# Transposing DMAs at steps 1 and 3, their joins at 5 and 7, in a mixture-of-experts block on one core

## The chip, the cores and the metric

The kernel runs on one core of a Trainium2 chip. The metric is the device time of one execution, in microseconds (us). PE is the matrix engine (its weight loads are listed apart, as PEld), DVE the vector engine, ACT the scalar engine, POOL the GpSimd engine. SP is a sequencer that here only issues DMAs; the rows of the profile call it SPq. All five run their own instructions in order and wait for each other through semaphores.

## The reference

One layer of a generator over 2048 tokens of width 1024, in float32: a short gated convolution mixer and a mixture of experts with expert-choice routing.

```python
hl = modulate(rms_norm(lat, norm_g[i, 0]), sh1, sc1)
gate_b, gate_c, v = jnp.split(hl @ w_in, 3, axis=-1)
lat = lat + g1 * ((gate_b * dwconv_centred(gate_c * v, conv_w)) @ w_out)
h = modulate(rms_norm(lat, norm_g[i, 1]), sh2, sc2)
...
cap = EC_CAPACITY_FACTOR * N // N_EXPERTS                 # 2 * 2048 // 16 = 256
aff = jax.nn.softmax((h @ w_router).astype(jnp.float32), axis=-1)
g, idx = lax.top_k(jnp.swapaxes(aff, 1, 2), cap)          # each of 16 experts takes 256 tokens
xs = h[idx]
hid = jax.nn.silu(xs @ w_gate) * (xs @ w_up)
ys = (hid @ w_down) * g                                    # added back to the chosen tokens' rows
lat = lat + g2 * scatter_add(ys, idx)
```

## The kernel before

**Arithmetic.** Every product is made of float32 operands that are split into a rounded high part and the rest (`ws[:, 0]` and `ws[:, 1]` for weights, `xT[:, 0]` and `xT[:, 1]` for tokens); high x high, high x low and low x high are three matmuls. ACT makes a high part by a copy (L200), DVE the low part by a subtraction (L210).

**The weight chain.** All weights go through one queue of pieces of 512 KB, in a fixed order: `load_to` issues the load of a piece on SP into one of three raw buffers (L184), `split_high` is ACT's copy, `split_low` DVE's subtraction, and `split_low(i)` then calls `load_to(i + 3)`, so a load goes out when the piece three before it has been split. A split piece stands in one of eight `ws` buffers until PE has used it.

**The output stage** (about 580 to 830 us) goes over 16 blocks of 128 tokens. Between the matmuls of block tb + 1, `behind(tb, k)` places the work on block tb at step k of 8: residual and norm at 0, transposition for the router at 4 and 5, `out_h2` at 5, `router_mm` at 7; the router's sum over halves (`router_sum`, a small PE product, L727) follows at step 0 of the next block. `out_h2` finishes a row block `u` of h on DVE and calls `halves_out`: ACT copies `u` apart into its 16-bit halves (L683) and SP stores them to `hhalf`, from which experts 1 to 15 gather. `router_mm` ends with ACT's copy of the router's sums out of PSUM into `lt` (L722), which `router_sum` reads.

**The experts** (from 880 us). Expert e runs as `gate_up(e, 0)`, `down(e - 1, 0)`, `gate_up(e, 1)`, `down(e - 1, 1)`: half of the hidden columns each, and the down products of the expert before between them. A `gate_up` has eight steps k (24 matmuls of 256 columns each, with one weight piece split for later), a `down` four steps kk (12 matmuls of 512 columns, one piece split). `gate_up` ends with silu on ACT (L1054), the product on DVE (L1055) and the split of the result; PE's next `gate_up` but one uses the same PSUM banks.

Tokens for expert e + 1 come in four pieces of work, which are placed at steps by the `between` functions:

- `pick_oh` and `pick`: from the chosen slots DVE builds a one-hot table, PE multiplies it (16 small matmuls), DVE makes the row numbers `idx`, and POOL issues two gathers of 128 rows each into `xs` (L984).
- `turn(e, s)`: SP issues a transposing DMA of half s of the tokens, `tr <- xs` (L1012). The buffer of half 1 is that of the one-hot table.
- `join(e, s)`: DVE copies one 16-bit half and ACT the other into `full` (L1018, L1019), ACT makes the high part of `xT` (L1022), DVE the low part (L1023).

Within a step of `gate_up` the order is: ACT's split of the step's piece, then `between(k)`, then DVE's split, which issues the next load. What is placed by `between` therefore stands on SP ahead of that load, and on ACT and DVE between two splits.

Of the kernel before, what the change touches and what calls it, by code (L numbers as in the profile page):

```python
# [20 lines left out]
E = 16  # L21
# [20 lines left out]
def block_kernel(ctx: ExitStack, tc, x, c, ada_w, ada_b, norm_g, w_in, conv, w_out, router, wg, wu, wd, out):  # L42
# [307 lines left out]
    with tc.tile_pool(name="mix", bufs=1) as mix:  # L350
# [7 lines left out]
        def hl_tile(shape, dt=F32R):  # L358
            return mix.tile(shape, dt, name="hl", tag="hl", bufs=16)
# [258 lines left out]
        def half(h):  # L618
            return slice(h * QT, (h + 1) * QT)
# [49 lines left out]
        def out_rms(tb):  # L669
            ss = ss_of.pop(tb)  # L670
            nc.gpsimd.tensor_add(ss[:, 2:3], ss[:, 0:1], ss[:, 1:2])
            nc.gpsimd.tensor_scalar(ss[:, 3:4], ss[:, 2:3], 1.0 / D, EPS, op0=ALU.mult, op1=ALU.add)
            r = small.tile([P, 1], F32, name="rstd", tag="rstd", bufs=6)
            nc.gpsimd.tensor_tensor(r, ss[:, 3:4], mhalf, op=ALU.pow)
            rn = small.tile([P, 1], F32, name="rneg", tag="rneg", bufs=6)
            nc.gpsimd.tensor_scalar(rn, r, -1.0, None, op0=ALU.mult)
            r_of[tb] = r, rn
            r_of_last[:] = [r]

        def halves_out(tb, u):  # L680

            uh = hl_tile([P, 2, D], U16)
            nc.scalar.activation(uh, u.bitcast(U16).rearrange("p (d h) -> p h d", h=2), AF.Copy)  # L683
            nc.sync.dma_start(hhalf[tb * P:(tb + 1) * P], uh)

        def out_h2(tb):
            xt, u = xt_of.pop(tb), u_of.pop(tb)
            for s in (half(0), half(1)):
                nc.vector.scalar_tensor_tensor(u[:, s], u[:, s], r_of[tb][0], sh2b[:, s], op0=ALU.mult, op1=ALU.add)
            halves_out(tb, u)  # L690
            nc.gpsimd.dma_start(hscr[tb * P:(tb + 1) * P, :], u)
            nc.gpsimd.dma_start(out[0, tb * P:(tb + 1) * P, :], xt)

# [13 lines left out]
        def router_t(tb, g):  # L707
            router_t_high(tb, g)
            router_t_low(tb, g)

        def router_mm(tb, k0=0, k1=KD):
            if k0 == 0:
                pl_of[tb] = tp.tile([2 * E, P], F32, name="plt", tag="tp")
            pt = pl_of[tb]
            hh, hl_ = hT_[tb]
            for k in range(k0, k1):
                w = rts[:, k].rearrange("p j e -> p (j e)")
                nc.tensor.matmul(pt, w, hh[:, k], start=(k == 0), stop=False)
                nc.tensor.matmul(pt, w, hl_[:, k], start=False, stop=(k == KD - 1))
            if k1 == KD:  # L720
                lt = small.tile([2 * E, P], F32, name="lt", tag="lt", bufs=2)
                nc.scalar.activation(lt, pt, AF.Copy)  # L722
                pl_of[tb] = lt

        def router_sum(tb):
            pl = tp.tile([P, E], F32, name="pl", tag="tp")
            nc.tensor.matmul(pl, pl_of[tb], fold, start=True, stop=True)  # L727
            pl_of[tb] = pl
# [44 lines left out]
        def behind(tb, k):  # L773

            if k == 0:
                if tb:
                    router_sum(tb - 1)
                for h in range(2):
                    out_res(tb, h)
                if tb:  # L780
                    router_sm(tb - 1)
                out_rms(tb)
                if tb:
                    router_gate(tb - 1)
            if k in (4, 5):
                router_t(tb, k - 4)
            if k == 5 and tb + 2 < NB:
                out_split(tb + 2)
            if k == 5:
                out_h2(tb)  # L790
            if k == 7:
                router_mm(tb)

        for tb in range(NB - 1):
            if tb + 2 < NB:
# [10 lines left out]
        tb = NB - 1  # L806
# [24 lines left out]
        xt, u, r = xt_of[tb], u_of[tb], r_of_last[0]  # L831
# [175 lines left out]
    def turn(e, s):  # L1007

        if s == 0:
            xT_of[e] = moe.tile([P, 2, KD, CAP], F32R, name="xT", tag="xT", bufs=2)  # L1010
        tr = tr_of[e, s] = moe.tile([P, 2 * KD, P], U16, name="tr", tag="oh" if s else "tr", bufs=1)
        nc.sync.dma_start_transpose(tr, xs_of[e][s])  # L1012

    def join(e, s):
        tr = tr_of.pop((e, s)).rearrange("p (h k) t -> p h (k t)", h=2)
        full = moe.tile([P, KD * P], F32, name="full", tag="full", bufs=1)
        both = full.bitcast(U16).rearrange("p (n h) -> p h n", h=2)
        nc.vector.tensor_copy(both[:, 0], tr[:, 0])  # L1018
        nc.scalar.activation(both[:, 1], tr[:, 1], AF.Copy)  # L1019
        f = full.rearrange("p (k t) -> p k t", t=P)  # L1020
        hi, lo = (xT_of[e][:, i, :, s * P:(s + 1) * P] for i in range(2))
        nc.scalar.activation(hi, f, AF.Copy)  # L1022
        nc.vector.tensor_sub(lo, f, hi.bitcast(F32))  # L1023

    def gate_up(e, fh, between=lambda k: None):
        xT = xT_of[e]
        if fh == 0:
            hT_of[e] = {}
        ps = [[mm.tile([P, 2, CAP], F32, name="pm", tag="mm") for _ in range(2)] for _ in range(2)]
        for kk in range(KD // 2):  # L1030
            for j in range(2):
                k = 2 * kk + j
                n = w_moe[0, e, fh, kk] + n_split - 2 + j
                if (e, fh) != (0, 1):
                    split_high(n)
                between(k)
                while n_done <= min(n, len(pieces) - 1):
                    split_low(n_done, nc.gpsimd if n_done % 2 and (e, fh) < (1, 1) else None)
                for f in range(4):
                    c0 = slice(f * P, (f + 1) * P)  # L1040
                    for m in range(2):
                        o = ps[m][f // 2][:, f % 2]
                        w = ws_of[w_moe[m, e, fh, kk]]
                        nc.tensor.matmul(o, w[:, 0, j, c0], xT[:, 0, k], start=(k == 0 and f % 2 == 0), stop=False,  # L1044
                                         skip_group_check=True)
                        nc.tensor.matmul(o, w[:, 0, j, c0], xT[:, 1, k], start=False, stop=False,  # L1046
                                         skip_group_check=True)
                        nc.tensor.matmul(o, w[:, 1, j, c0], xT[:, 0, k], start=False, stop=(k == KD - 1),  # L1048
                                         skip_group_check=True)
        hT = moe.tile([P, 2, 4, CAP], F32R, name="hT", tag="hT", bufs=4)  # L1050
        hT_of[e][fh] = hT
        for f2 in range(2):
            sg = moe.tile([P, 2, CAP], F32, name="sg", tag="sg", bufs=2)
            nc.scalar.activation(sg, ps[0][f2], AF.Silu)  # L1054
            nc.vector.tensor_mul(sg, sg, ps[1][f2])  # L1055
            t = slice(2 * f2, 2 * f2 + 2)
            nc.scalar.activation(hT[:, 0, t], sg, AF.Copy)
            nc.vector.tensor_sub(hT[:, 1, t], sg, hT[:, 0, t].bitcast(F32))
# [44 lines left out]
    def tick(k):  # L1103
        next(rounds, None)
# [11 lines left out]
    for e in range(E):  # L1116
        if e == 0:
            gate_up(0, 0, lambda k: (tick(k), pick(1) if k == 7 else None))
            gate_up(0, 1, lambda k: (turn(1, 0), turn(1, 1)) if k == 4 else join(1, k - 6) if k > 5 else tick(k) if 1 < k < 4 else None)
            continue  # L1120
        if e == 1:
            gate_up(1, 0, lambda k: tick(k) if k > 1 else None)
            down(0, 0, lambda kk: tick(kk) if kk else None)
            for _ in rounds:
                pass
            pick_oh(2)
            gate_up(1, 1, lambda k: pick(2) if k == 2 else None)
        else:
            if e + 1 < E:
                pick_oh(e + 1)  # L1130
            gate_up(e, 0)
            down(e - 1, 0, (lambda kk: pick(e + 1) if kk == 2 else None) if e + 1 < E else (lambda kk: None))
            gate_up(e, 1, (lambda k: (turn(e + 1, 0), turn(e + 1, 1)) if k == 4 else join(e + 1, 0) if k == 7 else None)
                    if e + 1 < E else (lambda k: None))
        if e == 1:
            down(e - 1, 1, lambda kk: (turn(2, 0), turn(2, 1)) if kk == 0 else join(2, kk - 2) if kk > 1 else None)
        else:
            down(e - 1, 1, (lambda kk: join(e + 1, 1) if kk == 0 else None) if e + 1 < E else (lambda kk: None))
    down(E - 1, 0)
    down(E - 1, 1)  # L1140

# [21 lines left out]
```

## Time and profile before

| | |
|---|---|
| median of 3 runs | 2103.72 us (2103.25 to 2105.81) |
| the profiled execution | 2107.72 us, of which the profile's span is 2105.6 |
| busy: PE, DVE, ACT, POOL | 1900.3, 1149.3, 818.4, 335.5 us |
| mean granted clock of PE | 0.953 |
| DMA | 368 MB, 175 GB/s mean |

A row of the timeline has the start, the duration, the engine, the line and operation, out<-in, the count, and in brackets how long the engine sat idle before and what ended that. A row of waits has who waited, for whom, the sum in us, how often, and the longest. A stretch has its length and then each engine's busy time with its number of instructions, the granted clock, the share of DMA and GB/s.

### The profile page before, as it was taken

The numbers are of one execution on the slowest core, as the hardware profiler recorded it, in microseconds if no ns is written. First come the engines' busy times: TensorE is split into PE (matmuls) and PEld (weight loads), VectorE is DVE, ScalarE is ACT, GpSimd is POOL, SyncE is SP. The second block draws the span as 40 slices with busy tenths as digits, with TensorE's granted clock in tenths as the row PEclk, the third lists the DMA queues.
The fourth block names the chain that finished last, engine by engine and source line by source line (L and its number), as shares of the span: only waits on it lengthen the run. The fifth ranks groups of instructions, "written<-read, shape, count | busy, mean of one in ns | idle before, by whom it ended". The sixth has DMA issues, their size and how long they took to land.

```text
span 2105.6 us, 29363 instructions
## 1 busy us (share of the span) xinstructions
PE 1900.3 (90%) x11690; PEld 1677.2 (80%) x11690; DVE 1149.3 (55%) x1656; ACT 818.4 (39%) x1066; POOL 335.5 (16%) x521
## 2 busy tenths in 40 slices
PE   4999999999999997489999888988988988988988
PEld 3888888888877775389898888987977978987887
DVE  7544334444356656866655655655655655565454
ACT  3411135111234434454444444444444444444442
POOL 3310011100112223332101110110110110111001
PEclk8999999999999998689999999999999999999999
DMA  9343242342255453455778677776776867866765
GB/s 289 103 140 125 85 136 85 131 150 65 66 180 190 164 196 113 137 171 190 204 200 236 198 200 213 220 186 194 231 190 200 239 182 211 238 180 196 225 197 143
DMA packets 281277, 368.49 MB, mean 175 GB/s; under 512 B 74748, under 2 KB 156724, under 8 KB 281140
## 3 DMA queue, kind: packets, MB, share of 16 engines
q1 hardware_dynamic: 265172, 308.94, 48.0%
q0 software_dynamic: 15968, 57.68, 10.2%
q8 instruction: 91, 1.49, 0.3%
q14 instruction: 46, 0.38, 0.1%
HBM read 300.51 MB, written 50.33 MB: 167 GB/s over the span
## 4 chain that ended last, share of the span: by engine, by line
PE 56%; DMA 15%; DVE 12%; ACT 9%; issue 7%; SPq 1%; POOL 1%; ACTq 0%; POOLq 0%; DVEq 0%
PE pm L439 8%; PE pm L440 8%; PE pm L442 8%; PE pm L1046 6%; PE pm L1048 6%; PE pm L1044 6%; DMA raw<-in_moe_w_gate_dram 5%; DVE ws L210 4%; DMA raw<-in_moe_w_up_dram 4%; ACT ws L200 3%; DMA raw<-in_moe_w_down_dram 3%; PE pm L1068 2%; PE pm L1066 2%; PE pm L1067 2%; PE pm L644 2%
## 5 line engine op out<-in xcount | busy, mean ns | idle before, releaser
L210 DVE TENSOR_TENSOR ws<-raw,ws 128x1024 fp32r<-128x1024 f32 x415 | 499.1, 1224 | 325.5 <-ACT ws L200 324.3
L1044 PE MATMUL pm<-xT,ws 128*128 128x256 f32 x2048 | 588.1, 287 | 89.9 <-ACT xT L1022 89.9
L200 ACT ACTIVATE ws<-raw 128x1024 fp32r<-128x1024 f32 x437 | 452.5, 1055 | 530.7 <-DMA raw<-in_moe_w_up_dram 208.4
L1046 PE MATMUL pm<-xT,ws 128*128 128x256 f32 x2048 | 585.7, 286 | 10.5 <-DVE xT L1023 10.4
L1048 PE MATMUL pm<-xT,ws 128*128 128x256 f32 x2048 | 582.5, 284 | 0.0
L1044 PEld LDWEIGHTS pm<-xT,ws 128*128 128x128 f32 x2048 | 402.9, 197 | 96.7 <-ACT xT L1022 96.1
L1046 PEld LDWEIGHTS pm<-xT,ws 128*128 128x128 f32 x2048 | 402.1, 196 | 15.8 <-DVE xT L1023 14.7
L1048 PEld LDWEIGHTS pm<-xT,ws 128*128 128x128 f32 x2048 | 401.8, 196 | 0.0
L439 PE MATMUL pm<-hl,ws 128*128 128x512 f32 x768 | 305.4, 398 | 0.9 <-ACT hl L389 0.9
L440 PE MATMUL pm<-hl,ws 128*128 128x512 f32 x768 | 301.5, 393 | 0.0
L1092 POOL DMA_INDIRECT out_dram<-ot,idx x32 | 105.8, 3305 | 713.0 <-DVE ot L1086 709.0
L442 PE MATMUL pm<-hl,ws 128*128 128x512 f32 x768 | 217.0, 391 | 0.3 <-DVE hl L392 0.3
L1068 PE MATMUL pm<-ws,hT 128*128 128x512 f32 x512 | 201.8, 394 | 0.0
L1066 PE MATMUL pm<-ws,hT 128*128 128x512 f32 x512 | 201.0, 393 | 0.0
L1067 PE MATMUL pm<-ws,hT 128*128 128x512 f32 x512 | 200.5, 392 | 0.0
L439 PEld LDWEIGHTS pm<-hl,ws 128*128 128x128 f32 x768 | 145.6, 190 | 31.6 <-ACT hl L389 1.3
L442 PEld LDWEIGHTS pm<-hl,ws 128*128 128x128 f32 x768 | 145.0, 189 | 31.2 <-DVE hl L392 0.7
L440 PEld LDWEIGHTS pm<-hl,ws 128*128 128x128 f32 x768 | 145.6, 190 | 30.3 <-issue 1.0
L452 DVE TENSOR_TENSOR u<-cs,pm 128x512 f32<-128x512 f32 x32 | 22.5, 703 | 231.4 <-ACT cs L449 231.4
L449 ACT ACTIVATE cs<-pm 128x512 f32<-128x512 f32 x32 | 19.1, 596 | 332.2 <-issue 261.3
L1067 PEld LDWEIGHTS pm<-ws,hT 128*128 128x128 f32 x512 | 96.2, 188 | 20.3
L1068 PEld LDWEIGHTS pm<-ws,hT 128*128 128x128 f32 x512 | 96.3, 188 | 20.0
(273 smaller groups left out, 2058.9 us busy)
## 6 DMA issues: line engine op xcount, KB each, us to landing
raw<-in_moe_w_gate_dram SPq DMA_DIRECT2D x128, 512.0 KB, 4.8
raw<-in_moe_w_up_dram SPq DMA_DIRECT2D x128, 512.0 KB, 4.8
raw<-in_moe_w_down_dram SPq DMA_DIRECT2D x128, 512.0 KB, 4.4
raw<-in_sc_w_in_dram SPq DMA_DIRECT2D x45, 512.0 KB, 4.9
xt<-in_x_dram SPq DMA_DIRECT2D x32, 512.0 KB, 7.2
aw<-in_ada_w_dram SPq DMA_DIRECT2D x32, 512.0 KB, 6.7
hl<-in_ada_w_dram SPq DMA_DIRECT2D x32, 256.0 KB, 5.4
hl<-vscr SPq DMA_DIRECT2D x16, 512.0 KB, 6.6
```

The source lines that it names most:

```text
L200: nc.scalar.activation(t[:, 0], raws[n_high], AF.Copy)
L210: (eng or nc.vector).tensor_sub(t[:, 1, ..., s], raw[..., s], t[:, 0, ..., s].bitcast(F32))
L439: nc.tensor.matmul(ps[m], wh, t[:, 0], start=(k == 0), stop=False)
L440: nc.tensor.matmul(ps[m], wl, t[:, 0], start=False, stop=False)
L442: nc.tensor.matmul(ps[m], W(k, m)[0], t[:, 1], start=False, stop=(k == KD - 1))
L1044: nc.tensor.matmul(o, w[:, 0, j, c0], xT[:, 0, k], start=(k == 0 and f % 2 == 0), stop=False, skip_group_check=True)
L1046: nc.tensor.matmul(o, w[:, 0, j, c0], xT[:, 1, k], start=False, stop=False, skip_group_check=True)
L1048: nc.tensor.matmul(o, w[:, 1, j, c0], xT[:, 0, k], start=False, stop=(k == KD - 1), skip_group_check=True)
L1066: nc.tensor.matmul(ps[s], h, w[:, 0, j], start=(k == 0), stop=False)
L1067: nc.tensor.matmul(ps[s], h, w[:, 1, j], start=False, stop=False)
L1068: nc.tensor.matmul(ps[s], l, w[:, 0, j], start=False, stop=(k == KD - 1))
L1092: st = nc.gpsimd.indirect_dma_start(out=out_rows, out_offset=bass.IndirectOffsetOnAxis(ap=idx_of[e][:, s:s + 1], axis=0), in_=ots[s], in_o ...
```

## The change

Three things are moved; no instruction is added or taken away.

1. In the experts, the two `turn`s of expert e + 1 stand at steps 1 and 3 of `gate_up(e, 1)` instead of both at step 4; `join(e + 1, 0)` stands at step 5 instead of 7, and `join(e + 1, 1)` at step 7 instead of step 0 of the `down` behind it. For experts 1 and 2, which are prepared in other places, turns and joins also move up by one or two steps.
2. `pick(e + 1)` stands at step 1 of `down(e - 1, 0)` instead of step 2.
3. In the output stage `halves_out` is called at step 7, behind `router_mm`, instead of at step 5 in `out_h2`.

```diff
+        u_last = []
+
         def out_h2(tb):
...
-            halves_out(tb, u)
+            u_last[:] = [u]
...
             if k == 7:
                 router_mm(tb)
+                halves_out(tb, u_last[0])
...
-            gate_up(0, 1, lambda k: (turn(1, 0), turn(1, 1)) if k == 4 else join(1, k - 6) if k > 5 else tick(k) if 1 < k < 4 else None)
+            gate_up(0, 1, lambda k: (tick(k), turn(1, k - 2)) if k in (2, 3) else join(1, k - 5) if k in (5, 6) else None)
...
-            gate_up(1, 1, lambda k: pick(2) if k == 2 else None)
+            gate_up(1, 1, lambda k: pick(2) if k == 2 else turn(2, k - 6) if k > 5 else None)
...
-            down(e - 1, 0, (lambda kk: pick(e + 1) if kk == 2 else None) if e + 1 < E else (lambda kk: None))
-            gate_up(e, 1, (lambda k: (turn(e + 1, 0), turn(e + 1, 1)) if k == 4 else join(e + 1, 0) if k == 7 else None)
+            down(e - 1, 0, (lambda kk: pick(e + 1) if kk == 1 else None) if e + 1 < E else (lambda kk: None))
+            gate_up(e, 1, (lambda k: turn(e + 1, k // 2) if k in (1, 3) else join(e + 1, k // 2 - 2) if k in (5, 7) else None)
                     if e + 1 < E else (lambda k: None))
         if e == 1:
-            down(e - 1, 1, lambda kk: (turn(2, 0), turn(2, 1)) if kk == 0 else join(2, kk - 2) if kk > 1 else None)
+            down(e - 1, 1, lambda kk: join(2, kk - 1) if kk in (1, 2) else None)
         else:
-            down(e - 1, 1, (lambda kk: join(e + 1, 1) if kk == 0 else None) if e + 1 < E else (lambda kk: None))
+            down(e - 1, 1)
```

What this does to the order on SP, in the second half of an expert from 2 on (raw is a weight piece's raw buffer, tr the transposed tokens, xs the gathered ones). Before:

```order
L184 DMA raw<-in_moe_w_down_dram 128x2x512 x4
L184 DMA raw<-in_moe_w_gate_dram 128x2x512
L1012 DMA_TRANSPOSE tr<-xs 128x16x128 x2
L184 DMA raw<-in_moe_w_up_dram 128x2x512
L184 DMA raw<-in_moe_w_gate_dram 128x2x512
```

And after, where line numbers are three higher:

```order
L184 DMA raw<-in_moe_w_down_dram 128x2x512 x2
L1015 DMA_TRANSPOSE tr<-xs 128x16x128
L184 DMA raw<-in_moe_w_down_dram 128x2x512 x2
L1015 DMA_TRANSPOSE tr<-xs 128x16x128
L184 DMA raw<-in_moe_w_gate_dram 128x2x512
```

The first transposing DMA has moved ahead of two loads of down weights and one of gate weights, the second ahead of the gate load; each now has a load just in front of it.

The order on ACT at the same place (L200 is a split, full and xT are the join, sg and hT the silu). Before:

```order
L200 ACTIVATE ws<-raw 128x1024 x12
L1019 ACTIVATE full<-tr 128x1024
L1022 ACTIVATE xT<-full 128x8x128
L1054 ACTIVATE sg<-pm 128x512
L1057 ACTIVATE hT<-sg 128x512
L1054 ACTIVATE sg<-pm 128x512
L1057 ACTIVATE hT<-sg 128x512
L1019 ACTIVATE full<-tr 128x1024
L1022 ACTIVATE xT<-full 128x8x128
L200 ACTIVATE ws<-raw 128x1024 x12
```

And after:

```order
L200 ACTIVATE ws<-raw 128x1024 x10
L1022 ACTIVATE full<-tr 128x1024
L1025 ACTIVATE xT<-full 128x8x128
L200 ACTIVATE ws<-raw 128x1024 x2
L1022 ACTIVATE full<-tr 128x1024
L1025 ACTIVATE xT<-full 128x8x128
L1057 ACTIVATE sg<-pm 128x512
L1060 ACTIVATE hT<-sg 128x512
L1057 ACTIVATE sg<-pm 128x512
L1060 ACTIVATE hT<-sg 128x512
L200 ACTIVATE ws<-raw 128x1024 x12
```

The first join now has two splits between it and the second, and the second stands ahead of the silus instead of behind them. DVE's parts move in the same way.

The order on ACT in a block of the output stage (hl<-u is the copy of halves, lt<-plt the copy of the router's sums, junk the squares of the norm). Before:

```order
L701 ACTIVATE hl<-pt 128x512 x2
L633 ACTIVATE hl<-hl 128x1024
L683 ACTIVATE hl<-u 128x2048
L722 ACTIVATE lt<-plt 32x128
L666 ACTIVATE junk,ss<-xt 128x512 x2
```

And after:

```order
L703 ACTIVATE hl<-pt 128x512 x2
L633 ACTIVATE hl<-hl 128x1024
L724 ACTIVATE lt<-plt 32x128
L683 ACTIVATE hl<-u 128x2048
L666 ACTIVATE junk,ss<-xt 128x512 x2
```

The two copies have changed places; the stores on SP and the DMAs on POOL keep their order.

## The prediction

> **What bounds the kernel now.** I read the page first, then who waits for whom, then the stretches of one expert, then the rows around the one wait that is left.
>
> ```profile
> span 2105.6 us, 29363 instructions
> PE 1900.3 (90%) x11690; PEld 1677.2 (80%) x11690; DVE 1149.3 (55%) x1656; ACT 818.4 (39%) x1066; POOL 335.5 (16%) x521
> ...
> raw<-in_moe_w_gate_dram SPq DMA_DIRECT2D x128, 512.0 KB, 4.8
> ...
> raw<-in_moe_w_down_dram SPq DMA_DIRECT2D x128, 512.0 KB, 4.4
> ...
> hl<-vscr SPq DMA_DIRECT2D x16, 512.0 KB, 6.6
> ```
>
> ```profile
> PEld pl L727 <- ACT lt L722: 25.9, 16, 2.3
> ...
> PE pm L1044 <- ACT xT L1022: 89.9, 15, 8.1
> ```
>
> PE is busy for 90%, and the waits that it keeps in the experts have one owner: the first product of each expert waits for the token tile xT, 15 times. The stretches of the expert that starts at 1240.92 (gate and up 0, down 0, gate and up 1, down 1, then the wait), and twelve experts together:
>
> ```profile
> 1240.92:1266.14 25.22, 24.54 (x192) 24.25 (x193) 17.16 (x19) 11.29 (x11) 7.62 (x3) 0.88 0.75 209
> 1266.14:1277.65 11.51, 11.51 (x66) 9.35 (x65) 6.00 (x8) 5.53 (x8) 0.00 (x0) 1.00 0.55 184
> 1277.65:1299.43 21.78, 21.78 (x193) 21.77 (x192) 12.52 (x15) 8.05 (x8) 1.97 (x2) 1.00 0.82 248
> 1299.43:1310.42 10.99, 10.99 (x50) 8.84 (x48) 2.44 (x3) 4.93 (x5) 0.00 (x0) 1.00 0.84 226
> 1310.42:1318.06 7.64, 0.16 (x1) 0.00 (x0) 5.07 (x8) 4.09 (x6) 0.00 (x0) 0.81 0.23 69
> ...
> 1089.73:2005.79 916.06, 825.99 (x5953) 768.77 (x5953) 518.76 (x589) 406.84 (x433) 115.04 (x60) 0.95 0.71 207
> ...
> 1018.99:1089.73 70.74, 69.03 (x496) 64.25 (x496) 38.57 (x46) 29.67 (x33) 7.32 (x5) 0.96 0.71 199
> ```
>
> First number: length in us; after PE, PEld, DVE, ACT and POOL comes the granted clock. Undisturbed, an expert takes 21.78 + 11.51 + 21.78 + 10.99 = 66.06 us. The wait adds 7.64, and the product behind it takes 25.22 instead of 21.78: it waits once more for the low half of xT, and its clock is 0.88 where it is 1.00 elsewhere. So one boundary costs 7.64 + 3.44 = 11.08 us. Twelve experts take 916.06, that is 76.34 each, 10.3 over 66.06.
>
> Why xT is late, at the same boundary:
>
> ```profile
> 1293.96 0.37 SPq L184 DMA_DIRECT2D raw<-in_moe_w_gate_dram  x1
> 1294.38 7.05 SPq L1012 DMA_TRANSPOSE tr<-xs  x2
> 1301.53 1.00 SPq L184 DMA_DIRECT2D raw<-in_moe_w_up_dram  x1
> ...
> 1312.29 0.37 SPq L184 DMA_DIRECT2D raw<-in_moe_w_gate_dram  x1
> ```
>
> ```profile
> 1306.43 1.06 ACT L200 ACTIVATE ws<-raw 128x1024 fp32r<-128x1024 f32 x1 [5.68 <-DMA raw<-in_moe_w_up_dram]
> 1307.39 1.36 ACT L1019 ACTIVATE full<-tr 128x1024 uint16<-128x1024 uint16 x1
> 1308.78 1.06 ACT L1022 ACTIVATE xT<-full 128x1024 fp32r<-128x1024 f32 x1
> 1309.74 0.58 ACT L1054 ACTIVATE sg<-pm 128x512 f32<-128x512 f32 x1
> ...
> 1315.38 1.33 ACT L1019 ACTIVATE full<-tr 128x1024 uint16<-128x1024 uint16 x1
> 1316.96 1.06 ACT L1022 ACTIVATE xT<-full 128x1024 fp32r<-128x1024 f32 x1 [0.24 <-DVE full L1018]
> ```
>
> The two transposes hold SP for 7.05 us; the up weights behind them are issued at 1301.53, so ACT idles 5.68 us; only then come the first join, the silus and, at 1315.38, the second join, whose end at 1318 is PE's start. PE had finished its gate and up product at 1299.43 already: ACT and DVE, fed by loads, run ten us behind PE. The load chain (three raw buffers; each load is issued when DVE has split the piece three before it) is a second limit close behind PE.
>
> What a transpose costs the queue (the first is shown alone, then the load ahead of it):
>
> ```profile
> L1012 SPq DMA_TRANSPOSE tr<-xs x1: 5040/5040/5040, 1294.4 to 1294.4; - x1
> ```
>
> ```profile
> L184 SPq DMA_DIRECT2D raw<-in_moe_w_gate_dram x1: 367/367/367, 1294.0 to 1294.0; - x1
> ...
> DMA to landing us min/median/max: 5.6/5.6/5.6
> ```
>
> 1294.38 + 5.04 = 1299.42, and the load ahead landed at 1293.96 + 5.6 = 1299.56: the transpose held SP until the load before it was in. The second took what is left of 7.05, 1.9.
>
> **The change, part by part.**
>
> *Turns to steps 1 and 3, joins to 5 and 7 (12 experts).* The transposes now stand behind the second and the fourth down load, each with a fresh load ahead, so I charge each the drain of that load (4.4). Walk of the same boundary with the medians above, ACT split 1.06, and DVE split and low half:
>
> ```profile
> 1311.01 1.22 DVE L210 TENSOR_TENSOR ws<-raw,ws 128x1024 fp32r<-128x1024 f32 x1
> ...
> 1318.04 1.23 DVE L1023 TENSOR_TENSOR xT<-full,xT 128x1024 fp32r<-128x1024 f32 x1 [1.18 <-ACT xT L1022]
> ```
>
> ```profile
> 1287.22 5.50 SPq L184 DMA_DIRECT2D raw<-in_moe_w_down_dram  x3
> ```
>
> Second down load 1287.2, in at 1291.6. First transpose 1287.6 to 1291.5. Third down load 1291.6, in at 1296.0; fourth at 1292.4 (no later than now: 1287.22 + 5.50 is its end), in at 1296.8. Second transpose 1292.8 to 1296.7. Gate load 1296.8 (now 1293.96), in at 1301.6. The third down piece is split by 1298.4, which issues the up load (now 1301.53), in at 1303.2. ACT splits the fourth at 1298.2, joins the first half until 1300.7; DVE's low half ends 1301.9, its split 1303.1. Gate piece split by ACT 1302.8, DVE 1304.4. Up piece: ACT 1304.4, second join until 1306.8, DVE low half 1308.0, split 1309.3: this issues the load that now goes out at 1312.29. First silu 1307.4, its product on DVE 1310.0. PE ends its down product at 1310.42 and finds everything: the 11.08 us are gone at this boundary.
>
> They do not stay gone. The load chain reached its marking load at 1309.3 instead of 1312.29 (3.0 earlier), and the second join (1315.38 to 1317.9, 2.5 us) no longer stands between the silus and the next splits. So the chain's own round is 5.5 us shorter, not 11: 76.34 - 5.5 = 70.8. That is above PE's 66.06, so after an expert or two PE is held by the chain, and it does not matter whether as one wait or as several short ones. I take 71.0, a little over, because the same bytes then come 7% faster. 12 x (76.34 - 71.0) = 64 us. Bounds: 66.06 (PE alone, 123 us) and 74.3 (chain gains 2 only, 24 us), both kept for the range. I take a middle value because the walk, whose every duration is a row, lands there.
>
> [...]
>
> *Picks one quarter earlier.* The same 16 matmuls and two gathers; POOL does nothing between, PE's pick stays in its 11.51.
>
> ```profile
> 1280.44 1.00 POOL L984 DMA_INDIRECT xs<-hhalf,idx  x1 [20.11 <-DVE gate L990]
> ...
> DMA to landing us min/median/max: 6.9/7.1/7.3
> ```
>
> They are issued when DVE, one split (1.2 us) earlier than now, reaches the index: in at about 1286.2 and 1287.8, against the transposes' turns at 1287.6 and 1292.8. So the new wait of SP on the gather is hidden, and it stays hidden while the transpose drains a load anyway. Price 0.
>
> *Experts 0 and 1.*
>
> ```profile
> 939.78 0.58 PE L1044 MATMUL pm<-xT,ws 128*128 128x256 f32 x1 [3.15 <-ACT xT L1022]
> ...
> 1018.99 0.58 PE L1044 MATMUL pm<-xT,ws 128*128 128x256 f32 x1 [3.95 <-ACT xT L1022]
> ```
>
> Both boundaries carry the 3.44 as well: 6.6 and 7.4. Turns move up two steps, joins one, worth at least one weight split of ACT and DVE (about 2.3) plus the wait for it: I count 5.5 (silus of the product just done take the rest) and 7.0; bounds 2 each to the whole. The expert behind, 70.74 now, starts without its 3.44 but with a later chain: 2.
>
> *The copy of halves behind the router's copy (output stage).*
>
> ```profile
> 676.43 1.91 ACT L683 ACTIVATE hl<-u 128x2048 uint16<-128x2048 uint16 x1 [2.62 <-DVE u L689]
> 678.25 0.25 ACT L722 ACTIVATE lt<-plt 32x128 f32<-32x128 f32 x1
> ```
>
> ```profile
> 676.76 0.62 PE L647 MATMUL pm<-ws,hl 128*128 128x512 f32 x2
> 678.55 0.39 PE L727 MATMUL pl<-fold,lt 32*128 32x16 f32 x2 [1.17 <-ACT lt L722]
> ```
>
> ```profile
> 678.80 0.53 SPq L623 DMA_DIRECT2D hl<-vscr  x1
> ```
>
> ```profile
> 687.41 1.05 ACT L633 ACTIVATE hl<-hl 128x1024 fp32r<-128x1024 f32 x1
> ```
>
> ACT is idle 2.62 us ahead of the 1.91 us copy while the router's product is done; the small copy, 0.25, waits behind. Put first, it fits into that idle time, and the big copy starts when it starts now. PE's second L647 started 0.23 after the first (10.99 / 48 for such a product), at 676.99, so the next could start at 677.2: 1.34 us for each of 13 blocks and about 2 for each of two longer ones, 20.5 (the table of waits has 25.9 for the weight loads, the longest 2.3). Bounds 0 and 21. What is late next: the vscr load is issued behind the halves' store and takes 6.6 (the page); the split that needs it starts 8.6 after the issue now and would start 7.3 after it, still behind the landing.
>
> **Sum.** 64 + 2 + 7 + 5.5 + 20.5 = 99 us. The profiled execution took 2107.72 (span 2105.6), the median of the runs is 2103.72, 4 less; taken off the median: 2005.
>
> **Rivals.**
> 1. *PE becomes the only limit.* Loads come sooner in the smoother order, experts take 66 to 69: 88 to 123 us from the twelve, 1981 down to 1946. For it: the expert of 70.74 lost 3.44 at its start and hardly anything later, transposes included. Against: ACT and DVE end ten us behind PE in the expert shown.
> 2. *The drains eat the gain.* Each transpose now drains a load of its own and the down weights stand behind the first; the chain gains 2 a round: 24 + 8 + 20 = 52, 2052. For it: 5.04 and 1.9 become 4.4 twice. Against: ACT's 5.68 idle goes.
> 3. *Slower: SP stands at the first transpose until the gather is in.* Down loads, their splits and PE's down product queue behind it. A start up to 1289.6 costs nothing (the drain's end, 1291.5, less the 1.9 that a transpose takes alone), so the gather has 3.4 us; past that each us is one in the round. To end above now it would take 8.2 a round (5.3 + 35 / 12 from the other parts), a gather of some 18 us where these take 7. Then 2110 and up.
> 4. *The reordered copy gives nothing*, because the wait moves to the big copy: 2025.
>
> **How the numbers follow.** Forecast (experts of 69 to 73, 1981 to 2029) 0.62; rival 1 0.16; rival 2 0.13; rival 4 0.05; rival 3 0.03; no effect 0.01. The time is the forecast's, 2005. The range, 1962 to 2042, leaves out the far half of rival 1, rival 2's end and rival 3. A change below 0.2% (4 us) could not be told from none: faster 0.95, same 0.02, slower 0.03.
>
> **What would show it.** Right: the waits on xT L1022 fall from 89.9 to under 45, PE's wait on the router's copy to nearly nothing, blocks of the output stage 13.3 us instead of 14.65, experts near 71, each transpose on SP about 4.4. Wrong: transposes of 2 us or experts at 66 (rival 1); new PE waits in the down products behind ws (rivals 2 and 3).

## The result and the profile after

The changed kernel takes 2003.2 us (median of four, 2000.56 to 2004.91), the kernel before 2103.48 beside it (2102.17 to 2105.81): a ratio of 0.9521, with an interval from 0.9505 to 0.9537. The forecast was 2005.0. The profiled executions differ a little more, 2105.6 against 1998.8 of span, since the one before lay 4 us above its median and the one after 2.6 below. One execution of a kernel below, the profiled one of raw4_join_behind, took 3813.6 us where its four others took 1944; its time and its trace are not used.

The head of the page after (the engines have the instructions that they had; the 12 more in the first line, 29363 before, are semaphore instructions):

```profile
span 1998.8 us, 29375 instructions
...
PE 1885.4 (94%) x11690; PEld 1659.4 (83%) x11690; DVE 1151.3 (58%) x1656; ACT 820.8 (41%) x1066; POOL 343.7 (17%) x521
```

The table of waits, with the lines that answer to 25.9 for the router's copy and 89.9 for xT (who waited, for whom, us in total, times, longest):

```profile
PE pm L1047 <- DVE sg L1058: 14.7, 18, 1.2
...
PE pm L1049 <- DVE xT L1026: 4.9, 11, 0.9
...
PE pm L1047 <- ACT xT L1025: 2.6, 1, 2.6
...
PEld pl L729 <- ACT lt L724: 1.3, 3, 0.6
```

The wait on xT is gone but for one. In its place stand short ones: for the low half (L1049), and for the product behind silu (sg L1058), which frees the PSUM banks that the next product writes. Both belong to ACT and DVE, which still run behind PE.

The stretches after: twelve experts (answering to 916.06), then one expert in its four products (gate and up 0, down 0, gate and up 1, down 1):

```profile
1058.07:1897.48 839.41, 816.51 (x5954) 756.69 (x5952) 510.85 (x580) 402.55 (x426) 122.05 (x60) 0.99 0.78 225
1615.73:1641.40 25.67, 24.05 (x190) 23.39 (x191) 17.75 (x21) 9.91 (x11) 7.62 (x3) 0.93 0.68 197
1641.40:1652.90 11.50, 11.50 (x67) 9.41 (x67) 5.74 (x6) 5.64 (x7) 0.00 (x0) 1.00 0.83 237
1652.90:1674.70 21.80, 21.80 (x192) 21.71 (x192) 13.16 (x17) 9.17 (x11) 2.98 (x2) 1.00 0.84 250
1674.70:1685.95 11.25, 11.25 (x53) 9.27 (x51) 6.77 (x7) 9.24 (x9) 0.00 (x0) 1.00 0.75 228
```

839.41 / 12 = 69.95 us per expert instead of 76.34. There is no stretch of waiting any more; two products take their undisturbed time, the last 11.25 instead of 10.99, and the first one 25.67 instead of 21.78. The first experts of the twelve run at PE's own 66.06 (1058.07 to 1124.13 and on to 1190.19), then, as the lead of the weight chain is used up, each takes 69 to 72.

SP at the end of that expert (issues of loads and of the two transposes):

```profile
1663.04 2.38 SPq L184 DMA_DIRECT2D raw<-in_moe_w_down_dram  x2
1666.34 4.08 SPq L1015 DMA_TRANSPOSE tr<-xs  x1
1670.52 1.62 SPq L184 DMA_DIRECT2D raw<-in_moe_w_down_dram  x2
1672.23 4.00 SPq L1015 DMA_TRANSPOSE tr<-xs  x1
1676.32 0.54 SPq L184 DMA_DIRECT2D raw<-in_moe_w_gate_dram  x1
1676.95 0.42 SPq L184 DMA_DIRECT2D raw<-in_moe_w_up_dram  x1
1682.33 0.37 SPq L184 DMA_DIRECT2D raw<-in_moe_w_gate_dram  x1
...
L1015 SPq DMA_TRANSPOSE tr<-xs x30: 3610/4274/5419, 895.5 to 1882.4; - x30
```

The last line groups all 30 transposes: they hold SP for 4.27 us in the median, first and second alike.

ACT in the output stage, one block to the next:

```profile
668.95 0.27 ACT L724 ACTIVATE lt<-plt 32x128 f32<-32x128 f32 x1 [2.16 <-PE plt L721]
669.40 1.91 ACT L683 ACTIVATE hl<-u 128x2048 uint16<-128x2048 uint16 x1 [0.19 <-DVE u L691]
...
682.35 0.27 ACT L724 ACTIVATE lt<-plt 32x128 f32<-32x128 f32 x1 [2.16 <-PE plt L721]
```

The small copy runs in time that ACT idled before, and blocks are 682.35 - 668.95 = 13.40 us apart (14.65 before).

**Where the 106.8 us of the spans came from.** The first product of the output stage, ahead of all that was changed, before and then after:

```profile
589.82 0.50 PE L644 MATMUL pm<-ws,hl 128*128 128x512 f32 x1
```

```profile
587.86 0.42 PE L644 MATMUL pm<-ws,hl 128*128 128x512 f32 x1
```

These 2.0 us are spread between executions: in eleven other runs this product stood at 587.6 to 589.4, at 588.0 in the two with the old order. The output stage, from there to the last of the 16 router sums (832.65 and 809.07): 242.8 to 221.2 us, 21.6; the two other runs with the old order took 241.3 and 240.9, so some 20 of it are the copy's and the rest is spread. By the first products of the experts, experts 0 and 1 until expert 2 starts: 138.1 to 131.05, 7.1; expert 2: 0.9. Twelve experts: 76.65. The end: 1.5 lost. With 0.1 between the stages, 106.8.

### The profile page after: what moved, and what is told of

The parts are those of the page before. It is cut to its first block, busy times and chain, and to the rows that moved or that the text cites. A ratio compares the mean times of both kernels' runs of the same rounds, so it can differ in the third digit from the quotient of the medians.

```text
span 1998.8 us, 29375 instructions
## 1 busy us (share of the span) xinstructions
PE 1885.4 (94%) x11690; PEld 1659.4 (83%) x11690; DVE 1151.3 (58%) x1656; ACT 820.8 (41%) x1066; POOL 343.7 (17%) x521
## 4 chain that ended last, share of the span: by engine, by line
PE 58%; DMA 14%; DVE 12%; issue 7%; ACT 6%; SPq 2%; POOL 1%; POOLq 0%; ACTq 0%; DVEq 0%
PE pm L439 8%; PE pm L440 8%; PE pm L442 8%; PE pm L1051 5%; PE pm L1047 5%; PE pm L1049 5%; DVE ws L210 4%; DMA raw<-in_moe_w_gate_dram 4%; DMA raw<-in_moe_w_down_dram 4%; ACT ws L200 3%; DMA raw<-in_moe_w_up_dram 3%; PE pm L644 3%; PE pm L647 3%; PE pm L645 3%; PE pm L1071 2%
## 5 line engine op out<-in xcount | busy, mean ns | idle before, releaser
L200 ACT ACTIVATE ws<-raw 128x1024 fp32r<-128x1024 f32 x437 | 452.7, 1055 | 459.8 <-DMA raw<-in_moe_w_down_dram 202.0
L1047 PE MATMUL pm<-xT,ws 128*128 128x256 f32 x2048 | 580.1, 283 | 21.2 <-DVE sg L1058 14.7
L1049 PE MATMUL pm<-xT,ws 128*128 128x256 f32 x2048 | 575.2, 281 | 5.2 <-DVE xT L1026 4.9
L1051 PE MATMUL pm<-xT,ws 128*128 128x256 f32 x2048 | 574.2, 280 | 2.5 <-DVE ws L210 2.5
L1047 PEld LDWEIGHTS pm<-xT,ws 128*128 128x128 f32 x2048 | 392.1, 191 | 30.6 <-DVE sg L1058 19.3
L1049 PEld LDWEIGHTS pm<-xT,ws 128*128 128x128 f32 x2048 | 391.8, 191 | 9.0 <-DVE xT L1026 7.8
L1051 PEld LDWEIGHTS pm<-xT,ws 128*128 128x128 f32 x2048 | 391.9, 191 | 3.8 <-DVE ws L210 3.7
L1095 POOL DMA_INDIRECT out_dram<-ot,idx x32 | 101.2, 3163 | 636.9 <-DVE ot L1089 626.6
```

Of the source, the lines that this page charges most:

```text
L200: nc.scalar.activation(t[:, 0], raws[n_high], AF.Copy)
L1095: st = nc.gpsimd.indirect_dma_start(out=out_rows, out_offset=bass.IndirectOffsetOnAxis(ap=idx_of[e][:, s:s + 1], axis=0), in_=ots[s], in_o ...
```

## The experiments

The theory after the result: three raw buffers make the weight chain (load, ACT's split, DVE's split, next load) the limit of the experts, the transposes and joins lengthen it, and the output stage is a part of its own. The main rival: the transposes or joins hold PE by themselves. Each kernel was timed beside the kernel before on the same chip; the ratio is compared, since the kernel before itself took 2098 to 2105 us beside them. "Twelve" is the length of the stretch of twelve experts in the run's trace.

| run | median us | ratio, interval | twelve us |
|---|---|---|---|
| the change | 2003.2 | 0.9521, 0.9505 to 0.9537 | 839.4 |
| copy_only | 2083.15 | 0.9901, 0.9871 to 0.9930 | 916.0 |
| experts_only | 2020.08 | 0.9602, 0.9573 to 0.9630 | 844.1 |
| pick_late | 1997.92 | 0.9524, 0.9487 to 0.9562 | 837.3 |
| turns_only | 2045.97 | 0.9731, 0.9702 to 0.9761 | 888.0 |
| joins_only | 2027.18 | 0.9656, 0.9628 to 0.9683 | 863.1 |
| adjacent | 2023.31 | 0.9619, 0.9589 to 0.9649 | 863.4 |
| adj67 | 2058.57 | 0.9805, 0.9778 to 0.9831 | 897.4 |
| act_queue | 2069.22 | 0.9855, 0.9797 to 0.9912 | 901.3 |
| join_behind | 2000.34 | 0.9511, 0.9486 to 0.9537 | 840.1 |
| raw4 | 1944.43 | 0.9242, 0.9217 to 0.9266 | 792.7 |
| raw4_join_behind | 1944.67 | 0.9240, 0.9216 to 0.9264 | - |
| before_raw4 | 1972.80 | 0.9404, 0.9389 to 0.9420 | 792.7 |

### The parts: the copy of halves, the experts, the pick

The kernel before with the copy moved:

```diff
             if k == 7:
                 router_mm(tb)
+                halves_out(tb, u_last[0])
```

> The kernel before with one of the three moves alone: the copy of halves stands behind the router's copy. Theory: the output stage is a part of its own; the first product of expert 1's predecessor, expert 0, came 23.7 us earlier after the whole change (857.18 against 880.85), so this move alone gives 23.7 us: 2079.8. The prediction's term for it was 20.5: 2083. Rival: the experts, held by the weight chain, give part of it back, 2090 to 2103.

> The changed kernel with the copy of halves put back in front of the router's copy, the moves in the experts kept. Theory: 2003.2 + 23.7 = 2027 if the parts add up, with the twelve experts still at about 70.2 us each and the blocks of the output stage at 14.65 again. The prediction's own terms for the experts (64 + 2 + 7 + 5.5 = 78.5) give 2025. Rival: the experts' gain depends on how far ahead the weight chain is at their start, then the twelve differ from 842 us by more than 10.

The first gained 1% (0.7 to 1.3; 1% of 2103.5 is 21 us), the second 4% (84 us): 105 against the 100 of the whole, so they add up within their intervals, and the output stage gives nothing back. Of the 23.7 in the first theory some 3.6 were spread (2.0 ahead of the stage, 1.6 in it); the 20.5 agrees with the 1%. The twelve stay at 916.0 with the copy alone and fall to 844.1 without it.

The pick back at its old step:

```diff
-            down(e - 1, 0, (lambda kk: pick(e + 1) if kk == 1 else None) if e + 1 < E else (lambda kk: None))
+            down(e - 1, 0, (lambda kk: pick(e + 1) if kk == 2 else None) if e + 1 < E else (lambda kk: None))
```

> The changed kernel with the pick of the next expert's tokens back at step 2 of the down product. Theory A (the prediction's price of 0 hangs on the drain that hides the gather): at the expert that starts at 1616 the index is ready at 1658.1 and the first transposing DMA starts at 1666.34 and ends at 1670.42; with the index one split of DVE later (ready about 1663, gather in at about 1671) the transpose would end about 2.5 us later, and with the weight chain as the limit that is 12 x 2.5 = 30 us: 2033. Theory B (the place of the pick is free, since the transpose waits for the load ahead anyway): 2003, within 4.

Theory B: no difference. At an expert of this run POOL and SP read:

```profile
1652.60 1.00 POOL L987 DMA_INDIRECT xs<-hhalf,idx  x1 [20.28 <-DVE gate L993]
```

```profile
1658.50 4.52 SPq L1015 DMA_TRANSPOSE tr<-xs  x1
1663.11 1.05 SPq L184 DMA_DIRECT2D raw<-in_moe_w_down_dram  x2
```

This gather lands 5.9 us after its issue, at 1658.5, and the transpose starts with it and stands until 1663.02 (4.52 us, no longer than the others with a load ahead). In the changed kernel too SP stands for gathers, at 8 of 15 experts and for 1.0 us at most:

```profile
SPq L1015 <- DMA xs<-hhalf,idx: 4.2, 8, 1.0
```

In pick_late the same row has 5.7 us in 8 waits, and the time is the same. Theory A had the index ready 5 us later (about 1663 instead of 1658); DVE, which here had three pieces ready to split in a row, lost only one split (1.2 us).

### Turns alone, joins alone

```diff
-            gate_up(e, 1, (lambda k: turn(e + 1, k // 2) if k in (1, 3) else join(e + 1, k // 2 - 2) if k in (5, 7) else None)
+            gate_up(e, 1, (lambda k: turn(e + 1, k // 2) if k in (1, 3) else join(e + 1, 0) if k == 7 else None)
...
-            down(e - 1, 1)
+            down(e - 1, 1, (lambda kk: join(e + 1, 1) if kk == 0 else None) if e + 1 < E else (lambda kk: None))
```

and, for the joins alone (at 6 and 7, since the transposes stand at 4):

```diff
-            gate_up(e, 1, (lambda k: turn(e + 1, k // 2) if k in (1, 3) else join(e + 1, k // 2 - 2) if k in (5, 7) else None)
+            gate_up(e, 1, (lambda k: (turn(e + 1, 0), turn(e + 1, 1)) if k == 4 else join(e + 1, k - 6) if k in (6, 7) else None)
```

> The changed kernel with the transposing DMAs at steps 1 and 3, but the joins of experts 3 to 15 back where they stood: the first at step 7, the second behind the silus, at step 0 of the down product. The prediction split its 5.5 us per expert into 3.0 from the earlier loads and 2.5 from the second join. Theory: the joins' 2.5 x 12 = 30 us are lost: 2033, experts near 72.7, and PE waits again on xT. Rival 1: the early transposes carry it all: 2003. Rival 2: the place of the joins carries it all: 2003 + 64 = 2067.

> The changed kernel with both transposing DMAs of experts 3 to 15 at step 4, where they stood before, and the joins at 6 and 7, both ahead of the silus. Theory: the 3.0 per expert from the earlier loads are lost, 2.5 stay: 2003 + 36 = 2039, experts near 73.2. Rival: the place of the joins carries it all: 2003. And if DVE stands at the first join until the transpose lands, as it did with the two transposes at step 3 (39.1 us in 13 waits), it comes out later still: 2045 to 2060.

The stretch of the twelve with the early transposes alone, then PE's wait in that run; and the stretch with the joins alone:

```profile
1058.01:1946.03 888.02, 829.35 (x5953) 772.30 (x5951) 518.33 (x589) 406.10 (x433) 126.07 (x60) 0.96 0.74 214
```

```profile
PE pm L1047 <- ACT xT L1025: 52.0, 13, 5.9
```

```profile
1055.89:1919.00 863.11, 826.53 (x5954) 766.97 (x5952) 514.39 (x582) 404.01 (x427) 126.07 (x60) 0.98 0.75 219
```

Against 916.06: 28.0 us from the turns (2.3 per expert), 53.0 from the joins (4.4). Together 81, where both at once gave 76.65. So both rivals of turns_only fall, and its 2033 too (0.9731 of 2103.5 is 2047): the two edits are nearly independent, and the joins are the larger part (though the joins alone stand at 6 and 7 and not at 5 and 7, so the two do not make up the whole exactly). In joins_only DVE did stand at its first join for the transposes (27.7 us in 13 waits), as that expectation said, and it still came out faster than the 2039 forecast (0.9656 of 2103.5 is 2031).

### Both transposes together: is the hold of SP the cost?

```diff
-            gate_up(e, 1, (lambda k: turn(e + 1, k // 2) if k in (1, 3) else join(e + 1, k // 2 - 2) if k in (5, 7) else None)
+            gate_up(e, 1, (lambda k: (turn(e + 1, 0), turn(e + 1, 1)) if k == 3 else join(e + 1, k // 2 - 2) if k in (5, 7) else None)
```

In a second kernel, adj67, `join(e + 1, k - 6) if k in (6, 7)` takes the place of the joins at 5 and 7.

> The changed kernel with both transposing DMAs of an expert at step 3, one straight behind the other, the joins at 5 and 7 as they are. Theory: each transpose holds SP until the load ahead of it has landed (3.6 to 5.4 us), two that stand together pay that once and 1.9 for the second, so the weight chain's round is some 2 us shorter, and as the chain is what holds the experts at 70 to 71 us, twelve experts gain about 23: 1980, with experts of 68 to 69. Rival 1: the experts are held by the order on ACT and DVE and not by the loads: 2003. Rival 2: the first join waits for the later transpose, and the two joins crowd: slower than 2003 by up to 20.

> The two transposing DMAs together at step 3, as in the run that took 2023, with the joins at 6 and 7 instead of 5 and 7. In that run the transposes held SP for 6.1 us together instead of 8.1, as expected, but DVE stood at the first join for 3.0 us in each of 13 experts (39.1 in all), with the split that issues the next load behind it. Theory A (that wait is the loss): without it the experts go from 72.5 to 69.5 or a little under: 1985 to 2000. Theory B (one long hold of SP lets all three raw buffers run empty, and the restart costs what the second drain saved): 2020 to 2030 again, though DVE waits no more at the join.

In adjacent the holds became shorter, as expected (3.4 to 5.2 for the first, 1.9 to 2.9 for the second), and the experts 2 us longer. The theory of adjacent fell, and the time is that of its rival 2, 20 us over the changed kernel. DVE waited at the join in that run:

```profile
DVE full L1021 <- DMA tr<-xs: 39.1, 13, 4.4
```

Putting the joins later took that wait to 5.4 us and the time went up by another 2%: theory A of adj67 fell, and B named too little. SP, then ACT and DVE of adj67 at one expert:

```profile
1706.52 5.70 SPq L1015 DMA_TRANSPOSE tr<-xs  x2
1712.31 0.85 SPq L184 DMA_DIRECT2D raw<-in_moe_w_gate_dram  x1
1713.26 0.43 SPq L184 DMA_DIRECT2D raw<-in_moe_w_up_dram  x1
1713.78 0.42 SPq L184 DMA_DIRECT2D raw<-in_moe_w_gate_dram  x1
1722.50 0.37 SPq L184 DMA_DIRECT2D raw<-in_moe_w_up_dram  x1
```

```profile
1716.63 1.06 ACT L200 ACTIVATE ws<-raw 128x1024 fp32r<-128x1024 f32 x1 [5.26 <-DMA raw<-in_moe_w_gate_dram]
```

```profile
1712.54 0.75 DVE L1021 COPY full<-tr 128x1024 uint16<-128x1024 uint16 x1
1720.07 1.23 DVE L1026 TENSOR_TENSOR xT<-full,xT 128x1024 fp32r<-128x1024 f32 x1 [6.78 <-ACT xT L1025]
1721.21 1.22 DVE L210 TENSOR_TENSOR ws<-raw,ws 128x1024 fp32r<-128x1024 f32 x1
```

Two holes stand in a row. SP issues no load for 5.70 us; all three buffers have run empty by then, three loads go out at once, and DVE, already inside the join of step 6, waits 6.78 us for ACT, which first has to split the gate piece that was just loaded. The split that frees the next buffer stands behind it, and no load is issued from 1713.78 to 1722.50. With the turns one step later (joins_only) that gate load is out ahead of the transposes. So the length of SP's hold alone is not the price; what counts is how long free buffers get no load, holds and joins together. That is read from this one expert; the fourth buffer below tests it.

### The transposes from ACT's queue

```diff
-        nc.sync.dma_start_transpose(tr, xs_of[e][s])
+        nc.scalar.dma_start_transpose(tr, xs_of[e][s])
```

> The changed kernel with the transposing DMAs issued by ACT instead of SP. Theory A: a transpose holds the queue that issues it until the DMA ahead of it on that same queue has landed. ACT issues no other DMA here, so the first one goes out at once; SP is no longer held for 8.1 us per expert, the weight chain runs ahead and PE is the limit, experts of 66 to 67: 2003 - 12 x 3.5 = 1960. ACT pays its own issue and, at the second transpose, what is left of the first. Theory B: the hold is for all DMAs of the core or the DMA engines themselves, then ACT, with the splits behind it, is held for 4 us twice: 2003 to 2030. A rival of A: ACT, 3 us ahead of the gather at step 1, waits for it with splits behind: 1975 to 2000.

The time of theory A fell by over 100 us, and those of theory B and of A's rival by over 40. ACT at the second of a pair of transposes, the group of all, and a new wait of PE:

```profile
1485.52 9.40 ACTq L1015 DMA_TRANSPOSE tr<-xs  x1
1495.48 1.06 ACT L200 ACTIVATE ws<-raw 128x1024 fp32r<-128x1024 f32 x1 [8.91 <-DMA raw<-in_moe_w_down_dram]
...
L1015 ACTq DMA_TRANSPOSE tr<-xs x30: 1334/3917/9397, 895.1 to 1947.0; - x30
...
DMA to landing us min/median/max: 5.3/10.7/20.1
```

```profile
PE pm L1070 <- DVE ws L210: 29.0, 12, 4.2
```

The trace names a load as the end of the 8.91, but 9.40 us after 1485.52 is 1494.92: what ACT stood behind is its own transposing DMA. The first of this pair was issued at 1481.49 and landed 13.7 us later, at 1495.2: the second held ACT until the first was in, with the weight splits behind. So in this pair A's rule of the hold stands; its time left out how long the first takes to land, 13.7 us here. The second held ACT for 3.1 to 9.4 us, the first for 1.3 to 1.5 us in every second expert and for 3.8 to 4.6 in the others; why it alternates was not tried.

### The join behind the split of its step

```diff
                 while n_done <= min(n, len(pieces) - 1):
                     split_low(n_done, nc.gpsimd if n_done % 2 and (e, fh) < (1, 1) else None)
+                behind_(k)
...
+                gate_up(e, 1, lambda k: turn(e + 1, k // 2) if k in (1, 3) else None,
+                        lambda k: join(e + 1, k // 2 - 2) if k in (5, 7) else None)
```

> The changed kernel with each join of experts 3 to 15 behind the split on DVE of its step instead of ahead of it; turns and steps unchanged. In the runs before, a join stands between ACT's and DVE's split of one piece, so the next load is issued only after the join (in the changed kernel at 1676 to 1688 us the split of a piece that ACT had at 1677.5 ends at 1682.2, and the one that ACT had at 1682.6 ends at 1687.6). Theory (the weight chain holds the experts at 70 to 71, and what counts is how long raw buffers stand empty): two loads per expert go out some 3.7 us earlier, the chain's round is about 3 us or more shorter: experts 66 to 68, 1953 to 1977. Rival (the transposes' holds alone make the bubble, the joins are hidden in it): 2003, within 4. Rival 2: DVE's low half of xT comes one split (1.2 us) later and PE waits for it: 2003 + 12.

No change: 0.9511, its interval on top of the other's. The loads do go out earlier, and then stop for longer. SP in this run:

```profile
1680.39 0.37 SPq L184 DMA_DIRECT2D raw<-in_moe_w_up_dram  x1
1681.52 0.37 SPq L184 DMA_DIRECT2D raw<-in_moe_w_gate_dram  x1
1690.06 0.37 SPq L184 DMA_DIRECT2D raw<-in_moe_w_up_dram  x1
```

The second join and the silus keep ACT and DVE from 1680.0 until 1688.8; all three buffers have been loaded by then, so an earlier load has no room. That this is why nothing was gained is read from this one expert.

### A fourth raw buffer

```diff
+        if more and i % 4 == 3:
+            t = more[0].tile([P] + shape, F32, name="rawm", tag="rawm", bufs=1)
...
-            load_to(i + n_raw)
+            load_to(i + n_raw + len(more))
...
-            ot_of[e] = [moe.tile([P, D], F32, name="ot", tag="ot", bufs=3) for _ in range(2)]
+            ot_of[e] = [moe.tile([P, D], F32, name="ot", tag="ot", bufs=2) for _ in range(2)]
```

`more` holds the experts' pool once they begin; every fourth piece then goes to the new buffer, and each load is issued four pieces ahead.

> The changed kernel with a fourth raw buffer in the expert stage (loads go out four pieces ahead instead of three; two instead of three output tiles make the room). Theory: with one more load ahead, the chain is no limit any longer: PE alone, experts of 66.06, 12 x (70.2 - 66.06) = 50 us: 1953. Rival 1: a transpose waits until all loads ahead have landed, with more of them in flight the holds grow and the restart is as empty as now: 1985 to 2003. Rival 2: the order on ACT and DVE at the end of a product (join, split, silu) holds PE, not the loads: 2003.

> Both: the fourth raw buffer and the joins behind DVE's split of their step. Theory: PE alone is the limit, 66.06 per expert with the first products undisturbed: 1953, no better than the better of the two single edits if that one reaches PE's own time, and near 1953 if neither does alone. Rival: what is left of PE's waits is the place of the silus behind the last split and join: 1975 to 1990.

> The kernel before, all of its order unchanged, with the fourth raw buffer in the expert stage (and two output tiles instead of three). Theory (what held the experts was the weight chain with three buffers, and the order of transposes and joins mattered only because it made that chain longer): the twelve experts fall from 76.5 to 66.06 each here too, 125 us; the output stage keeps its blocks of 14.65 and the first two boundaries some of their waits: 1965 to 1980, that is 20 to 35 above the changed kernel with four buffers. Rival (the late second join holds PE by itself, whatever the loads do): PE's waits on xT stay at 3 to 7 us per expert, 2003 to 2050.

The twelve experts of raw4 and of before_raw4:

```profile
1053.70:1846.42 792.72, 792.72 (x5954) 742.97 (x5952) 515.71 (x588) 401.78 (x433) 127.19 (x60) 1.00 0.82 239
```

```profile
1079.80:1872.52 792.72, 792.72 (x5953) 742.96 (x5952) 515.80 (x589) 402.68 (x432) 129.42 (x60) 1.00 0.80 239
```

792.72 / 12 = 66.06: PE never stops and its clock is 1.00 throughout, with the new order and with the old one alike. The transposes hold SP as long as ever, 4.24 us in the median beside 4.27 in the changed kernel:

```profile
L1019 SPq DMA_TRANSPOSE tr<-xs x30: 3161/4240/5068, 895.5 to 1821.8; - x30
```

So all that the change gained in these twelve experts, it gained because there were three buffers; the rivals of raw4 and of before_raw4, by which transposes, joins or silus hold PE whatever the loads do, fall. With four, what stays of the change is 26 us of span (1969.1 against 1942.9): the output stage and the first boundaries. raw4 is the fastest kernel of the study, 59 us under the change, 46.7 of them in the twelve experts; the joins behind the split add nothing to it.

## Why the prediction was right, and where it was off

- **What bounds it.** Right, and now shown: the weight chain is a second limit close behind PE, and one more buffer removed it (66.06 us per expert in raw4). The forecast that experts start at 66 and fall back to about 71, as several short waits, is what the trace after shows (66.06 twice, then 69 to 72).
- **Turns and joins, 64 us at 71.0 per expert.** Measured 76.65 at 69.95. The mis-sized term is the split of the 5.5: 3.0 for the earlier load and 2.5 for the join; the runs gave 2.3 and 4.4. The 2.5 counted ACT's two pieces of the second join; DVE's low half (1.23), which stands ahead of DVE's next split as well, was left out. With it the join's part would be 3.7 of the 4.4; that this is the reason is argued, not shown, and the rest stays open.
- **The price of a transpose**, 4.4 us each with a load ahead: 4.27 measured, in the median, where a load of expert weights held SP for 0.37. But the walk's silent premise, that the chain grows by what SP is held, holds only for this order: adjacent held SP less (6.1 us for the two where the changed kernel has 8.1) and was 20 us slower.
- **Pick, 0:** right, at either step, but without the margin of the prediction, by which the gather is in 1.4 us ahead of the transpose (1286.2 against 1287.6): SP does stand for it, 4.2 us in all, and the time until the load ahead has landed hides that.
- **Experts 0 to 2, 5.5 + 7.0 + 2 = 14.5:** 8.0 measured. The boundary from expert 0 to 1 gave 6.1 (72.0 to 66.0 us from second half to second half). The term that failed is the 7.0 at the boundary from expert 1 to 2: measured the same way it took 75.4 before and 74.4 after. PE still waits 2.64 us there, and the clock is 0.52 in the 7 us behind it. In seven other runs with that order and three buffers it took 69.5 to 74.1, so 1 to 6 us are to be had there; what decides how much was not tried.
- **The output stage, 20.5:** 21.6, some 20 of them the copy's, with blocks of 13.40 where 13.3 was said. The term's own parts, 13 x 1.34 and 2 x 2, add up to 21.4 and not to 20.5.
- **The sum.** 99 forecast against 106.8 of span: 12.7 more in the twelve experts, 6.5 less at experts 0 to 2, 1.1 more in the output stage and 2.0 more ahead of it (both mostly spread), 1.5 less at the end. The medians lie 100.3 apart, because the profiled executions lay 4.2 above and 2.6 below theirs. So that 2005 and 2003.2 lie 2 us apart is luck: the terms were off by up to 12.7 and made up for each other. The signs that were named did come: waits on xT 2.6, on the router's copy 1.3, experts of 69.95.
- **The rivals.** PE as the only limit holds for the first two of the twelve experts alone. SP standing for the gather came, but for at most 1.0 us of the 3.4 that the prediction had as free. The drains that eat the gain, and the waits in the down products that were to show them, did not come: PE's waits for split weights in the experts came to 3.2 us in all. The copy that gives nothing is refused by the 1% of copy_only.

## What to carry to other kernels

Before reordering what stands between two loads, ask how many buffers the chain of loads has: with three, holds of the issuing queue and copies between two splits cost PE time here, and moving them was worth 77 us in twelve experts; with a fourth buffer, the same moves were worth nothing there and PE ran at its own rate (66.06 us per expert). Holds did not add up by their length (adjacent held SP for 6.1 us instead of 8.1 and was 20 us slower): look for the time in which a free buffer gets no load, from all engines in the chain together. A small copy that another engine waits for goes ahead of a large one that nobody waits for soon (0.27 and 1.91 us here, some 20 us over the 16 blocks).

## What the runs showed of the hardware that was not expected

**A transposing DMA and its queue.** On SP it held the queue until the DMA ahead on that queue had landed. In the kernel before, the ten transposes behind a load whose landing the trace has end their hold within 0.2 us of it. Two in a row did nearly the same: in the kernel before, the second's hold ended within 0.7 us of the first's landing in the nine pairs whose first landing the trace has. A pair of adj67 (the first alone; landing counts from the issue, the hold included):

```profile
L1015 SPq DMA_TRANSPOSE tr<-xs x1: 3561/3561/3561, 1706.5 to 1706.5; - x1
...
DMA to landing us min/median/max: 5.6/5.6/5.6
```

The first lands at 1706.52 + 5.6 = 1712.1, and the second holds SP until 1706.52 + 5.70 = 1712.22. So the short hold of the second, 2.1 us here and 1.9 to 2.9 in adjacent, is, in this pair, what the first still took to land once its own hold was over. From ACT's queue it was the same in most pairs, with longer times: of the eleven there whose first landing the trace has, the second's hold ends within 0.8 us of it in eight, and 1.3 to 3.6 us after it in three, for which no cause was found; nor was one for the first's own hold of 1.3 to 4.6 us, with no DMA ahead of it on ACT.

Behind its hold the first one above took 2.0 us more to land (5.6 less 3.56), where loads of the same 512 KB took 4.3 to 4.5 from issue to landing (medians in adj67). In act_queue the median transpose took 10.7 us from issue to landing, the loads 4.5 to 5.1 (medians as well).

**The clock after short waits.** PE after the change, at the start of an expert, the stretch behind it, and the whole first product of another expert:

```profile
1615.73 0.39 PE L1047 MATMUL pm<-xT,ws 128*128 128x256 f32 x1 [0.34 <-ACT sg L1057]
1616.51 0.38 PE L1049 MATMUL pm<-xT,ws 128*128 128x256 f32 x1 [0.39 <-DVE xT L1026]
...
1618.24 0.39 PE L1047 MATMUL pm<-xT,ws 128*128 128x256 f32 x1 [1.23 <-DVE sg L1058]
```

```profile
1619.00:1623.00 4.00, 4.00 (x21) 3.75 (x21) 3.05 (x5) 3.13 (x5) 0.00 (x0) 0.57 0.37 130
1826.69:1853.19 26.50, 23.30 (x193) 22.46 (x194) 17.85 (x22) 10.97 (x12) 7.61 (x3) 1.00 0.67 197
```

No single wait is over 1.3 us, yet the granted clock falls to 0.57 behind these three, of 0.34, 0.39 and 1.23 us within 3 us. Behind the wait of 2.64 us ahead of expert 2 it was 0.52. But the expert at 1826.69 starts with almost the same waits (0.28, 0.39, 1.23), and its clock stays at 1.00: what decides was not found. Nor is the clock what makes the first product long: that one takes 26.50 us at full clock, and the one at 1615.73, counted to the same product, 25.93.
